# A two-layer decoder trunk on one core: input pieces between weight chunks, the second half of q and k two blocks later, and products in column groups

## The chip, the cores and the metric

The kernel runs on one core of one Trainium2 chip. A core has TensorE (PE, with its weight loads as PEld), VectorE (DVE), ScalarE (ACT), GpSimd (POOL) and SyncE (SP, which here only issues DMAs). The metric is the device time of one execution in microseconds. Before the change the median of 3 runs is 256.97 us (256.9 to 258.04).

## What is computed

Input and output are x of 1 x 256 x 1024 in f32. Two layers are applied one after another; each is one RMS norm, one input projection, two groups of heads side by side, and one output projection onto the residual:

```python
def hybrid_layer(x, norm_g, w_in, conv_w, conv_b, rg_wr, rg_br, rg_wi, rg_bi, rg_lam,
                 q_g, k_g, pe_k, w1_k, w2_k, pe_v, w1_v, w2_v, w_out):
    h = rms_norm(x, norm_g)
    z = h @ w_in
    ...
    y_a = rg_lru(causal_depthwise_conv(rg_x, conv_w, conv_b), rg_wr, rg_br, rg_wi, rg_bi, rg_lam)
    y_a = y_a * jax.nn.silu(rg_gate)
    y_b = nsa(q, k_c, v_c, k_s, v_s, k_w, v_w, br_gate, q_g, k_g,
              pe_k, w1_k, w2_k, pe_v, w1_v, w2_v)
    y_b = y_b * jax.nn.silu(nsa_gate)
    y = jnp.concatenate([y_a, y_b], axis=-1)
    return x + y @ w_out
```

`rg_lru` is a gated linear recurrence over the 256 tokens (512 channels). `nsa` is attention of 8 query heads on 2 key/value heads with three branches: compressed blocks (keys and values through a small MLP), selected blocks and a sliding window, each a masked softmax, mixed by sigmoid gates. q and k are normalised by head and partly rotated.

## The kernel before, in words

Everything is kept with channels on partitions and the 256 tokens in the free dimension, apart from q, k and v, which are made with tokens on partitions (two halves of 128). Each f32 operand of a large product is split into a high part that TensorE takes as fp32r and a low part, the rest; `mm3` (L170 to L173) issues three products for each tile: high by high, and the two mixed ones. The high part of a weight chunk (`wh`) is cast by ACT from the loaded `raw` (L165) or, for chunks with `dma=True`, by a DMA that POOL issues (L156); the low part (`wl`) is a subtraction on DVE (L166).

The weights come in 33 chunks a layer, and the program walks over them as steps: 8 of `tm1` (q, k and the keys, two token halves by 2 x 384 columns, so 12 products of 128 x 384 each), 2 of `cmp_prod`, 3 of `tm2` (values and gates), 12 of `fm` (blocks x0 to x3, n0, n1, g0 to g3, n2, n3, each 24 products of 128 x 256), and 8 of `out_proj`. A step has work placed before it, in its middle and after it. `SL` says ahead of which fm block the attention's parts stand: `qk` for `qk_transpose` of the two token halves, `cmp` for the compressed MLP (`cmp_act`, `cmp_kv`, `cmp_kt`), `att` for the scores and `turn`, `aout` for transposes and outputs, `gates` for the recurrence. `ahead(n)` says how many chunks beyond the next are cast and split early. From that the framework makes one instruction order per engine; PE, DVE, ACT, POOL and SP each run theirs in order and wait for each other by semaphores. PSUM has the pools s (3 banks), fm (2), pp (2) and m (1).

What the change touches:

- The start: `x_load` (L98) issues pieces of x on SP, between `Chunk.load` (L145) of the first chunks; chunk 0 comes in two halves. PE runs eight warm-up products (L113) meanwhile. `first_x(k)` makes piece k of h: the scaled high part on ACT (L213), the low part on DVE (L214), the square for the norm on ACT (L219, L222) and its addition on DVE (L223). `softplus` (L186 to L207) is a chain of small DVE steps. `rms1` needs the sum of all squares (L305), then DVE (L306 to L310) and POOL's power (L177); after it come `norm_sums` and `norm_rope`, which lead to q and k.
- `qk_transpose(t)`: two transposes of k on PE (L366), four copies on ACT (L370, L371) and two subtractions on DVE (L372, `kl`), then four transposes of q (L375), two copies (L379), two subtractions (L380, `qs`) and one copy (L382, `qT`). The scores (L570 to L572) of token half 0 need half 0 alone; those of half 1 need both. `cmp_hid` (L454) and `cmp_act` (L463 to L467: product, tanh `hth` on ACT, `hs` on DVE) lead to `cmp_kv` (L472, L473).
- `att_out(i)`: products with the values of the two branches, in groups of 64 columns (L619, L622), then one 128-wide product with the compressed values (L624), then DVE's product with the gate. It runs four times a layer.

```python
def ahead(n):
    return 0 if n < 4 else 1 if n < 7 else 2 if n % 33 < 14 or n % 33 > 26 else 1
...
    for n in range(RAWB):
        upto("load", n + 1)
        if n < 3:
            x_load(*((1, 3), (3, 5), (5, 8))[n])
```

Of the kernel before, what the change touches and what calls it, by code (L numbers as in the profile page):

```python
# [2 lines left out]

# [1 line left out]

# [5 lines left out]
F32 = mybir.dt.float32  # L11
# [3 lines left out]
AF = mybir.ActivationFunctionType  # L15
ALU = mybir.AluOpType
AX = mybir.AxisListType

P = 128
# [19 lines left out]
for _n, _w in (("g", 8), ("cw", 16), ("cb", 4), ("br", 4), ("bi", 4), ("lam", 4)):  # L39
# [10 lines left out]
PRB = 6  # L50

K = dict(scale="A", ev1="A", hid="A", pct="A")
SL = dict(qk=(0, 0), order=("x0", "x1", "x2", "x3", "n0", "n1", "g0", "g1", "g2", "g3", "n2", "n3"),
          cmp=(2, 3, 4), att=(1, 3, 3, 4, 6, 7, 10, 11), turn=(2, 4, 5, 6, 8, 10,
          12, 13), cs=(5, 5), cpt=6, aout=(6, 7, 12, 15), gates=(2, 3, 4, 5), tab=6, sqrt=5,
          scan=8, rout=(9, 11))
# [1 line left out]


def ahead(n):  # L60
    return 0 if n < 4 else 1 if n < 7 else 2 if n % 33 < 14 or n % 33 > 26 else 1

# [7 lines left out]
def hybrid_trunk_kernel(ctx: ExitStack, tc: tile.TileContext, vx, wc, wt, wv, wf, wo, w1, w2, pe,  # L72
# [56 lines left out]
    mhalf = cp.tile([P, 1], F32, name="mhalf")  # L129
    G.memset(mhalf, -0.5)  # L130
    warm = cp.tile([P, 1], F32, name="warm")
    A.activation(warm, ones, AF.Tanh)
    identb = cp.tile([P, P], BF16, name="identb")
    maskb = cp.tile([P, P], BF16, name="maskb")

# [1 line left out]
    class Chunk:  # L137
        def __init__(self, src, k, n, parts=1, dma=False):
            self.src, self.k, self.n, self.parts, self.dma = src.rearrange("p k n -> p (k n)"), k, n, parts, dma

        def cuts(self):
            w = self.k * self.n // self.parts
            return [slice(q * w, (q + 1) * w) for q in range(self.parts)]

        def load(self):  # L145
            self.raw = wp.tile([P, WCH], F32, name="raw", tag="raw", bufs=RAWB)[:, :self.k * self.n]
            for c in self.cuts():
                nc.sync.dma_start(self.raw[:, c], self.src[:, c])

        def high(self):  # L150
            self.wh = wp.tile([P, WCH], F32R, name="wh", tag="wh", bufs=WHB)[:, :self.k * self.n]
# [6 lines left out]
        def split(self):  # L158
            if not self.dma:
                self.high()  # L160
            hi = self.wh
            lo = wp.tile([P, WCH], F32R, name="wl", tag="wl", bufs=WLB)[:, :self.k * self.n]
            for c in self.cuts():
                if not self.dma:
                    A.copy(hi[:, c], self.raw[:, c])  # L165
                V.tensor_tensor(lo[:, c], self.raw[:, c], hi[:, c].bitcast(F32), op=ALU.subtract)  # L166
            self.hi, self.lo = (z.rearrange("p (k n) -> p k n", k=self.k) for z in (hi, lo))


# [84 lines left out]
    def layer(l, prev):  # L254
# [8 lines left out]
        def begin():  # L263
            if l == 0:
                L.h, L.sq = h_tiles(), act([P, S], "pct")
            else:
                L.h, L.sq = prev.nh, prev.nsq
            L.rc = act([P, 5, 4], "rc")
            L.rb = act([P, 2, S], "rb")
            L.acc1 = [(bank("s", 3), bank("s", 3)), (bank("s", 3), bank("pp", 2))]  # L270
            L.accc = bank("fm", 2)
            L.qT = act([P, 4, S], "qT")
            L.qs = act([P, 8, S], "qs", 1, F32R)
            L.kd = act([P, 2, 2, S], "kd2", 1, F32R)
            L.vv = act([P, NT, 2, P], "vv")
            L.gate = act([P, NT, 4, 2, 3], "gate")

        def first_x(k):
            h_split(0, L.h, k)
            if k == 2:  # L280
                nc.sync.dma_start(cst, consts)
                L.ga = tables(0)
            if k == 4:
                V.tensor_copy(identb, ident)
                V.tensor_copy(maskb, cview("mask"))
                L.tabs = tables2(L.ga)
            if k:
                sq_add(L.sq, k)
            if k == 5:
                L.sp = softplus()  # L290

# [69 lines left out]
        def qk_transpose(t):  # L361
            zn = L.zn[t]
            tok = slice(t * P, (t + 1) * P)
            pk = bank("pp", 2)
            for i in range(2):
                T.transpose(pk[:, i * P:(i + 1) * P],  # L366
                            zn[:, 8 + 2 * i:10 + 2 * i].rearrange("p h d -> p (h d)"), ident)
            for g in range(2):
                src = pk[g * HD:(g + 1) * HD, :2 * P].rearrange("p (b s) -> p b s", s=P)
                A.copy(L.kd[:HD, g, :, tok], src)  # L370
                A.copy(L.kd[HD:, g, :, tok], src)  # L371
                V.tensor_tensor(kl[:HD, g, :, tok], src, L.kd[:HD, g, :, tok].bitcast(F32), op=ALU.subtract)  # L372
            pq = bank("pp", 2)
            for i in range(4):
                T.transpose(pq[:, i * P:(i + 1) * P], zn[:, 2 * i:2 * i + 2].rearrange("p h d -> p (h d)"),  # L375
                            ident)
            for g in range(2):
                src = pq[g * HD:(g + 1) * HD].rearrange("p (i s) -> p i s", s=P)
                A.copy(L.qs[:HD, g::2, tok], src)  # L379
                V.tensor_tensor(L.qs[HD:, g::2, tok], src, L.qs[:HD, g::2, tok].bitcast(F32),  # L380
                                op=ALU.subtract)
            A.copy(L.qT[:, :, tok], pq.rearrange("p (i s) -> p i s", s=P))  # L382


# [229 lines left out]
        def att_out(i):  # L614
            pt = L.pts.pop(i)
            yb = L.yb = bank("m", 1)
            for b in range(2):
                for g in range(2):
                    T.matmul(yb[g * HD:(g + 1) * HD, :S], L.vv[:, 0, b, g * HD:(g + 1) * HD],  # L619
                             pt[:, g, b, 0:2].rearrange("p a s -> p (a s)"), start=(b == 0), stop=False)  # L620
                for g in range(2):
                    T.matmul(yb[g * HD:(g + 1) * HD, P:S], L.vv[:, 1, b, g * HD:(g + 1) * HD],  # L622
                             pt[:, g, b, 2], start=False, stop=False)
            T.matmul(yb[:, :S], L.vcb[:, 2 * i:2 * i + 2].rearrange("p g d -> p (g d)"), L.pct,  # L624
                     start=False, stop=True)
            yt = act([P, S], "tmp", 3)
            V.tensor_tensor(yt, yb[:, :S], L.sgn[:, i], op=ALU.mult)
            y_split(4 + i, yt)
# [157 lines left out]
        for i in range(2):  # L786
            at(SL["rout"][i], rg_out, 2 * i, mid=True)
        for n, (kind, j) in enumerate(order):
            step(Chunk(wf[l, base[kind] + j], KT, P, dma=n >= 4), R(fm, 0 if kind == "x" else j % 2),
                 F(post[kind], j), *plan[n])  # L790
        for half in range(2):
            for n in range(4):
# [7 lines left out]
        prev0 = prev0 or prev  # L800
        steps += st_
    ch = [s_[0] for s_ in steps]
    done = dict(load=0, cast=0, split=0)

    def upto(what, n):
        while done[what] < min(n, len(ch)):
            getattr(ch[done[what]], what)()
            done[what] += 1

    for n in range(RAWB):  # L810
        upto("load", n + 1)
        if n < 3:
            x_load(*((1, 3), (3, 5), (5, 8))[n])
    for n, (c, run, after, before, middle) in enumerate(steps):
        if n == 0:
            before[0]()
            before[2]()
            before = []
            upto("split", 1)
            sq_add(prev0.sq, 0)  # L820
        for f in before:
            f()
        if n < 4:
            upto("split", n + 2)
        upto("load", min(n + LOAD + 1, done["split"] + RAWB))
        upto("cast", n + CAST + 1)
        for f in middle:
            f()
        run(c)
        if after:  # L830
            after()
        upto("split", n + 2 + ahead(n))
# [108 lines left out]
```

## Time and profile before

| | before |
|---|---|
| median of 3 runs | 256.97 us |
| the profiled execution, its own time | 256.85 us |
| span in the profile | 255.1 us |
| PE busy | 245.7 us, 96% |
| PEld busy | 226.4 us, 89% |
| DVE busy | 198.0 us, 78% |
| ACT busy | 164.8 us, 65% |
| POOL busy | 41.3 us, 16% |
| moved by DMA | 57.17 MB, mean 224 GB/s |

The span is the time between the first and the last event of the profiled execution; the execution's own time is 1.75 us more. Busy time of PE counts matmuls whose ends are modelled, and weight loads (PEld) run beside them. The page's share of an engine is an average over stages, so the stages are read from the timeline and from windows.

### The profile page before, as it was taken

The page shows a single profiled execution, that of the slowest core. Times are in us where ns is not written, and L with a number is a line of the kernel's source. Part 1 is how long each engine was busy: PE and PEld are TensorE (multiplying, and loading weights), DVE is VectorE, ACT ScalarE, POOL GpSimd, SP SyncE. Part 2 cuts the span into 40 slices and gives each one's busy share as a digit, 9 for nine tenths or more (in the row PEclk, how much of TensorE's full clock was granted, in tenths as well). Part 3 has the DMA queues.
Part 4 walks back from the last instruction along what each step waited for, and adds up shares of the span by engine and source line. Part 5 has one row for each costly group of instructions (what it writes and reads, how often), then busy time and mean ns, then how long its engine had stood idle before and what let it go on. Part 6 is the DMA issues. An engine that isn't in the chain of part 4 may idle for free.

```text
span 255.1 us, 5220 instructions
## 1 busy us (share of the span) xinstructions
PE 245.7 (96%) x1954; PEld 226.4 (89%) x1954; DVE 198.0 (78%) x398; ACT 164.8 (65%) x419; POOL 41.3 (16%) x65
## 2 busy tenths in 40 slices
PE   8799998999999999999999999899999999999994
PEld 4699998898988998999999999688898979989993
DVE  4897789999978988754995569997986998865422
ACT  5966439889999878622864444679799896951000
POOL 0027461001800011100001053101100001010000
PEclk9999999999999999999999999999999999999999
DMA  6988999865794798662469868784457366842022
GB/s 203 335 272 282 350 416 363 303 177 211 247 328 166 247 279 276 176 197 76 156 220 360 296 218 252 274 297 168 163 169 226 130 220 237 272 154 82 3 82 82
DMA packets 17449, 57.17 MB, mean 224 GB/s; under 512 B 2192, under 2 KB 3088, under 8 KB 16912
## 3 DMA queue, kind: packets, MB, share of 16 engines
q1 hardware_dynamic: 12816, 40.06, 45.4%
q0 software_dynamic: 4608, 16.78, 21.3%
q8 instruction: 15, 0.25, 0.4%
q14 instruction: 10, 0.08, 0.1%
HBM read 55.78 MB, written 1.05 MB: 223 GB/s over the span
## 4 chain that ended last, share of the span: by engine, by line
PE 84%; DVE 8%; DMA 2%; ACT 2%; POOL 2%; issue 1%; SPq 0%; DVEq 0%; POOLq 0%
PE fm L173 14%; PE fm L171 14%; PE fm L172 14%; PE s L172 5%; PE s L171 4%; PE s L173 4%; PE pp L609 4%; PE m L619 3%; DVE wl L166 3%; PE fm L648 3%; PE s L570 2%; PE m L624 2%; DMA head<-in_vx_dram 2%; PE s L571 2%; PE m L622 1%; PE pp L171 1%
## 5 line engine op out<-in xcount | busy, mean ns | idle before, releaser
L166 DVE TENSOR_TENSOR wl<-raw,wh 128x1024 fp32r<-128x1024 f32 (+4 forms) x67 | 74.3, 1115 | 9.8 <-PE fm L173 4.6
L173 PE MATMUL fm<-hh,wl 128*128 128x256 f32 x192 | 55.8, 291 | 0.7 <-DVE wl L166 0.7
L171 PE MATMUL fm<-hh,wh 128*128 128x256 f32 x192 | 56.3, 293 | 0.0
L172 PE MATMUL fm<-hl,wh 128*128 128x256 f32 x192 | 55.3, 288 | 0.0
L165 ACT CAST wh<-raw 128x768 fp32r<-128x768 f32 (+4 forms) x35 | 30.8, 886 | 28.8 <-DMA raw<-in_wc_dram 7.0
L173 PEld LDWEIGHTS fm<-hh,wl 128*128 128x128 f32 x192 | 36.7, 191 | 1.4 <-DVE wl L166 0.9
L171 PEld LDWEIGHTS fm<-hh,wh 128*128 128x128 f32 x192 | 36.8, 192 | 0.3
L172 PEld LDWEIGHTS fm<-hl,wh 128*128 128x128 f32 x192 | 36.7, 191 | 0.1
L171 PE MATMUL fm<-yy,wh 128*128 128x256 f32 x96 | 27.7, 289 | 0.0
L583 ACT ACTIVATE pr<-s,sm 128x128 f32<-128x128 f32 (+1 forms) x64 | 26.2, 421 | 1.6 <-DVE sm L575 0.8
L173 PE MATMUL fm<-yy,wl 128*128 128x256 f32 x96 | 26.8, 279 | 0.0
L172 PE MATMUL fm<-yy,wh 128*128 128x256 f32 x96 | 26.8, 279 | 0.0
L596 ACT ACTIVATE pr<-pr,sm 128x128 f32<-128x128 f32 (+1 forms) x64 | 24.1, 454 | 1.9 <-DVE sm L589 1.9
L156 POOL DMA_DIRECT2D wh<-in_wo_dram x16 | 8.5, 530 | 68.4 <-PE fm L173 40.1
L172 PEld LDWEIGHTS fm<-yy,wh 128*128 128x128 f32 x96 | 18.1, 188 | 0.1
L171 PEld LDWEIGHTS fm<-yy,wh 128*128 128x128 f32 x96 | 18.1, 188 | 0.1
L173 PEld LDWEIGHTS fm<-yy,wl 128*128 128x128 f32 x96 | 18.0, 188 | 0.0
L171 PE MATMUL s<-wh,hh 128*128 128x384 f32 x48 | 16.0, 357 | 1.7 <-ACT wh L165 1.7
L156 POOL DMA_DIRECT2D wh<-in_wf_dram x16 | 9.0, 565 | 50.4 <-PE fm L173 26.9
L714 DVE TENSOR_TENSOR head<-head,fm 128x512 f32<-128x512 f32 x11 | 7.5, 685 | 12.1 <-PE fm L173 12.1
L172 PE MATMUL s<-wl,hh 128*128 128x384 f32 x48 | 16.4, 342 | 0.1
L173 PE MATMUL s<-wh,hl 128*128 128x384 f32 x48 | 16.1, 335 | 0.0
(202 smaller groups left out, 627.1 us busy)
## 6 DMA issues: line engine op xcount, KB each, us to landing
raw<-in_wf_dram SPq DMA_DIRECT2D x24, 512.0 KB, 4.8
wh<-in_wf_dram POOLq DMA_DIRECT2D x16, 512.0 KB, 4.4
raw<-in_wo_dram SPq DMA_DIRECT2D x16, 512.0 KB, 4.6
wh<-in_wo_dram POOLq DMA_DIRECT2D x16, 512.0 KB, 4.3
raw<-in_wt_dram SPq DMA_DIRECT2D x15, 384.0 KB, 3.5
yy<-in_w_dram SPq DMA_DIRECT2D x4, 1024.0 KB, 7.7
raw<-in_wc_dram SPq DMA_DIRECT2D x4, 512.0 KB, 5.1
raw<-in_wv_dram SPq DMA_DIRECT2D x4, 420.0 KB, 4.6
```

Source lines behind the costliest of these rows:

```text
L156: G.dma_start(self.wh, self.src)
L165: A.copy(hi[:, c], self.raw[:, c])
L166: V.tensor_tensor(lo[:, c], self.raw[:, c], hi[:, c].bitcast(F32), op=ALU.subtract)
L171: T.matmul(o, lh, rh, start=start, stop=False)
L172: T.matmul(o, lh, rl, start=False, stop=False)
L173: T.matmul(o, ll, rh, start=False, stop=stop)
L583: A.activation(pr[g][:, b], ov[:, b], AF.Exp, bias=sm[:, 0, 2 * g + b:2 * g + b + 1], accum_out=sm[:, 1, 2 * g + b:2 * g + b + 1])
L596: A.activation(pr[g][:, b], pr[g][:, b], AF.Copy, scale=sc_)
L609: T.transpose(pp[:, (2 * g + b) * P:(2 * g + b + 1) * P], pr[g][:, b, c * P:(c + 1) * P], ident)
L619: T.matmul(yb[g * HD:(g + 1) * HD, :S], L.vv[:, 0, b, g * HD:(g + 1) * HD], pt[:, g, b, 0:2].rearrange("p a s -> p (a s)"), start=(b == 0) ...
L648: T.matmul(pg[:, e * S:(e + 1) * S], L.rws[:, j, e], cx[:, j], start=True, stop=True)
L714: V.tensor_tensor(x_sb[:, m], x_sb[:, m], os_[0].rearrange("p (a s) -> p a s", a=2), op=ALU.add)
```

## The change

1. At the start, the first half of chunk 0 is issued on ACT's queue, ahead of the warm-up tanh. x comes in smaller pieces on SP: (0,1), half chunk, (1,2), chunk 1, (2,3), chunk 2, (3,5), chunk 3, (5,8), chunk 4.
2. The squares for the norm are taken later: pieces 0 to 7 at k = 2, 3, 3, 4, 5, 6, 7, 7 in place of each at its own k.
3. `qk=(0, 2)`: the second token half's `qk_transpose` stands before fm block x2 instead of x0.
4. `ahead` ends its value 2 at chunk 12 of a layer instead of 14, and the low parts of fm blocks 2 and 3 (4 and 5) are ordered on DVE behind the last `qs` of token half 0 (1).
5. The last product of `att_out` is issued as two groups of 64 columns.

```diff
-SL = dict(qk=(0, 0), order=("x0", "x1", "x2", "x3", "n0", "n1", "g0", "g1", "g2", "g3", "n2", "n3"),
+SL = dict(qk=(0, 2), order=("x0", "x1", "x2", "x3", "n0", "n1", "g0", "g1", "g2", "g3", "n2", "n3"),
...
-    return 0 if n < 4 else 1 if n < 7 else 2 if n % 33 < 14 or n % 33 > 26 else 1
+    return 0 if n < 4 else 1 if n < 7 else 2 if n % 33 < 12 or n % 33 > 26 else 1
...
-    A.activation(warm, ones, AF.Tanh)
...
+            self.after = None
...
-        def load(self):
+        def load(self, first=False):
             self.raw = wp.tile([P, WCH], F32, name="raw", tag="raw", bufs=RAWB)[:, :self.k * self.n]
-            for c in self.cuts():
-                nc.sync.dma_start(self.raw[:, c], self.src[:, c])
+            for q, c in enumerate(self.cuts()):
+                (A if first and q == 0 else nc.sync).dma_start(self.raw[:, c], self.src[:, c])
...
-                V.tensor_tensor(lo[:, c], self.raw[:, c], hi[:, c].bitcast(F32), op=ALU.subtract)
+                done = self.after() if self.after else None
+                with tc.issue_after(done.ins) if done else nullcontext():
+                    V.tensor_tensor(lo[:, c], self.raw[:, c], hi[:, c].bitcast(F32), op=ALU.subtract)
...
-            if k:
-                sq_add(L.sq, k)
+            for j in {2: [0], 3: [1, 2], 4: [3], 5: [4], 6: [5], 7: [6, 7]}.get(k, []):
+                sq_add(L.sq, j)
...
-                V.tensor_tensor(L.qs[HD:, g::2, tok], src, L.qs[:HD, g::2, tok].bitcast(F32),
-                                op=ALU.subtract)
+                L.qk_done[t] = V.tensor_tensor(L.qs[HD:, g::2, tok], src, L.qs[:HD, g::2, tok].bitcast(F32),
+                                               op=ALU.subtract)
...
-            T.matmul(yb[:, :S], L.vcb[:, 2 * i:2 * i + 2].rearrange("p g d -> p (g d)"), L.pct,
-                     start=False, stop=True)
+            for g in range(2):
+                T.matmul(yb[g * HD:(g + 1) * HD, :S], L.vcb[:, 2 * i + g], L.pct, start=False, stop=True)
...
-            step(Chunk(wf[l, base[kind] + j], KT, P, dma=n >= 4), R(fm, 0 if kind == "x" else j % 2),
+            c = Chunk(wf[l, base[kind] + j], KT, P, dma=n >= 4)
+
+            if n in (2, 3, 4, 5):
+                c.after = (lambda t: lambda: L.qk_done[t])(0 if n < 4 else 1)
+            step(c, R(fm, 0 if kind == "x" else j % 2),
...
-    done = dict(load=0, cast=0, split=0)
+    ch[0].load(True)
+    A.activation(warm, ones, AF.Tanh)
+    done = dict(load=1, cast=0, split=0)
...
-    for n in range(RAWB):
+    for n in range(1, RAWB):
+        x_load(*((1, 2), (2, 3), (3, 5))[n - 1])
         upto("load", n + 1)
-        if n < 3:
-            x_load(*((1, 3), (3, 5), (5, 8))[n])
+    x_load(5, 8)
...
-            sq_add(prev0.sq, 0)
```

How the instructions move. First SP's queue at the start of the program, before (head is the tile that holds the vectors and x; 256 columns are one piece of x):

```order
L100 DMA head<-in_vx_dram 128x336
L148 DMA raw<-in_wt_dram 128x384 x2
L100 DMA head<-in_vx_dram 128x512
L148 DMA raw<-in_wt_dram 128x768
L100 DMA head<-in_vx_dram 128x512
L148 DMA raw<-in_wt_dram 128x768
L100 DMA head<-in_vx_dram 128x768
L148 DMA raw<-in_wt_dram 128x768 x4
```

and now:

```order
L100 DMA head<-in_vx_dram 128x336
L148 DMA raw<-in_wt_dram 128x384
L100 DMA head<-in_vx_dram 128x256
L148 DMA raw<-in_wt_dram 128x768
L100 DMA head<-in_vx_dram 128x256
L148 DMA raw<-in_wt_dram 128x768
L100 DMA head<-in_vx_dram 128x512
L148 DMA raw<-in_wt_dram 128x768
L100 DMA head<-in_vx_dram 128x768
L148 DMA raw<-in_wt_dram 128x768 x3
```

One half of chunk 0 is gone from SP (it is on ACT's queue), and chunk 1 (the first 128 x 768) stands behind one further piece of x instead of two.

Second, DVE in layer 1 around the q,k stage, before:

```order
L166 TENSOR_TENSOR wl<-raw,wh 128x1024 x2
L400 TENSOR_SCALAR gate<-gate 128x24
L166 TENSOR_TENSOR wl<-raw,wh 128x1024
L400 TENSOR_SCALAR gate<-gate 128x24
L372 TENSOR_TENSOR kl<-pp,kd_1771 64x2x128
L380 TENSOR_TENSOR qs<-pp,qs 64x4x128
L372 TENSOR_TENSOR kl<-pp,kd_1771 64x2x128
L637 TENSOR_TENSOR xpad_71<-fm,rb 128x256
L380 TENSOR_TENSOR qs<-pp,qs 64x4x128
L166 TENSOR_TENSOR wl<-raw,wh 128x1024
```

and now (line numbers are by 2 to 4 higher: kl L375, qs L383, wl L168, xpad L640):

```order
L403 TENSOR_SCALAR gate<-gate 128x24 x2
L375 TENSOR_TENSOR kl<-pp,kd_1776 64x2x128
L383 TENSOR_TENSOR qs<-pp,qs 64x4x128
L375 TENSOR_TENSOR kl<-pp,kd_1776 64x2x128
L640 TENSOR_TENSOR xpad_71<-fm,rb 128x256
L383 TENSOR_TENSOR qs<-pp,qs 64x4x128
L168 TENSOR_TENSOR wl<-raw,wh 128x1024
L643 SCALAR_TENSOR_TENSOR cx<-xpad_71,head,cx 128x256
L168 TENSOR_TENSOR wl<-raw,wh 128x1024
```

The three low parts that stood ahead of the first kl are those of blocks x2, x3 and n0; x2's and x3's now stand behind the first token half's four steps, and n0's behind the second half's.

Third, ACT in the same stage, before (kd and qs are copies of k and q, hid and hth belong to the compressed MLP, L583 are exponentials of scores, L638 is the convolution's first step):

```order
L379 CAST qs<-pp 64x4x128
L370 CAST kd_1771<-pp 64x2x128
L371 CAST kd_1771<-pp 64x2x128
L83 COPY hid<-m 128x128
L379 CAST qs<-pp 64x4x128
L382 COPY qT<-pp 128x4x128
L583 ACTIVATE pr,sm<-s,sm 128x128 x4
L638 ACTIVATE cx<-xpad_72,head 128x256
L465 ACTIVATE hth<-m 128x160
L651 ACTIVATE rr<-fm,hb 128x256
L596 ACTIVATE pr<-pr,sm 128x128 x4
```

and now (L586 exponentials, L599 their scaling, L468 hth):

```order
L641 ACTIVATE cx<-xpad_71,head 128x256
L385 COPY qT<-pp 128x4x128
L83 COPY hid<-m 128x128
L586 ACTIVATE pr,sm<-s,sm 128x128 x4
L373 CAST kd_1776<-pp 64x2x128
L641 ACTIVATE cx<-xpad_72,head 128x256
L599 ACTIVATE pr<-pr,sm 128x128 x4
L374 CAST kd_1776<-pp 64x2x128
L382 CAST qs<-pp 64x4x128
L468 ACTIVATE hth<-m 128x160
L373 CAST kd_1776<-pp 64x2x128
```

The second half's copies stand behind the first tile's exponentials, and hth behind the scaling and three of these copies.

## Rows read from the trace of the kernel before

**Rows 1.** The page, parts 1 and 4: busy time by engine; the chain by engine.

```profile
PE 245.7 (96%) x1954; PEld 226.4 (89%) x1954; DVE 198.0 (78%) x398; ACT 164.8 (65%) x419; POOL 41.3 (16%) x65
...
PE 84%; DVE 8%; DMA 2%; ACT 2%; POOL 2%; issue 1%; SPq 0%; DVEq 0%; POOLq 0%
```

**Rows 2.** Waits of PE, first and last of six: us in total, times, longest.

```profile
PE s L171 <- ACT wh L165: 1.7, 1, 1.7
...
PE m L527 <- DVE sc L521: 0.3, 1, 0.3
```

**Rows 3.** The page's GB/s by slice, DMA issues to 24 us, timeline at the start.

```profile
GB/s 203 335 272 282 350 416 363 303 177 211 247 328 166 247 279 276 176 197 76 156 220 360 296 218 252 274 297 168 163 169 226 130 220 237 272 154 82 3 82 82
...
raw<-in_wt_dram SPq DMA_DIRECT2D x7, 384.0 KB, 5.3
...
6.99 0.51 ACT L213 ACTIVATE hh<-head 128x256 fp32r<-128x256 f32 x1 [1.85 <-DMA head<-in_vx_dram]
...
7.26 0.34 PE L173 MATMUL pp<-wh,hl 128*128 128x384 f32 x1
...
9.28 0.79 PE L171 MATMUL s<-wh,hh 128*128 128x384 f32 x3 [1.68 <-ACT wh L165]
```

**Rows 4.** Timeline of DVE from 7 us, and PE before the first fm block.

```profile
7.53 0.48 DVE L214 SCALAR_TENSOR_TENSOR hl<-head,hh 128x256 fp32r<-128x256 f32 x1 [1.59 <-ACT hh L213]
...
20.89 2.10 DVE L166 TENSOR_TENSOR wl<-raw,wh 128x768 fp32r<-128x768 f32 x2
23.52 0.16 DVE L306 TENSOR_SCALAR rc<-m 128x4 f32<-128x4 f32 x1 [0.53 <-PE m L305]
...
40.53 0.39 PE L173 MATMUL fm<-hh,wl 128*128 128x256 f32 x1 [0.67 <-DVE wl L166]
```

**Rows 5.** Timeline of layer 1's q,k stage, by engine; ACT at 180 us.

```profile
159.82 2.34 DVE L166 TENSOR_TENSOR wl<-raw,wh 128x1024 fp32r<-128x1024 f32 x2
...
163.38 0.41 DVE L372 TENSOR_TENSOR kl<-pp,kd 64x256 fp32r<-64x256 f32 x1
...
163.56 0.41 PE L454 MATMUL m<-yy,zz 128*32 128x128 f32 x2
165.18 0.41 PE L366 MATMUL pp<-cst,pt 128*128 128x128 f32 x2 [1.22 <-DVE kl L372]
165.52 1.52 PE L454 MATMUL m<-yy,zz 128*32 128x128 f32 x48
167.52 0.66 PE L375 MATMUL pp<-cst,pt 128*128 128x128 f32 x4 [0.48 <-ACT qT L382]
...
168.68 0.38 PE L570 MATMUL s<-kd,qs 128*128 128x256 f32 x1
...
180.48 0.47 ACT L651 ACTIVATE rr<-fm,hb 128x256 f32<-128x256 f32 x1 [1.55 <-PE fm L648]
```

**Rows 6.** Windows: us, PE, PEld, DVE, ACT, POOL busy, PE clock, DMA share, GB/s.

```profile
58.00:78.00 20.00, 19.85 (x153) 17.97 (x151) 18.40 (x50) 19.38 (x62) 7.14 (x12) 1.00 0.79 266
180.00:200.00 20.00, 19.75 (x151) 17.95 (x150) 16.54 (x47) 19.49 (x64) 1.63 (x3) 1.00 0.60 189
```

**Rows 7.** Timeline of ACT in layer 0: copies of the second token half.

```profile
48.18 0.37 ACT L370 CAST kd<-pp 64x256 fp32r<-64x256 f32 x1
...
48.96 0.58 ACT L379 CAST qs<-pp 64x512 fp32r<-64x512 f32 x1
```

**Rows 8.** Timeline of PE: the last products of att_out, at two places.

```profile
78.69 0.60 PE L619 MATMUL m<-pt,vv 128*64 128x256 f32 x4
79.12 0.39 PE L622 MATMUL m<-pt,vv 128*64 128x128 f32 x4
...
80.10 0.28 PE L173 MATMUL fm<-hh,wl 128*128 128x256 f32 x1
...
81.62 0.65 PE L619 MATMUL m<-pt,vv 128*64 128x256 f32 x4
...
82.42 0.28 PE L171 MATMUL fm<-hh,wh 128*128 128x256 f32 x1
```

More of the change, by code (lines that the diff above doesn't have):

```diff
@@ L1 @@
 import math
-from contextlib import ExitStack
+from contextlib import ExitStack, nullcontext
 import numpy as np
@@ L276, in begin @@
             L.gate = act([P, NT, 4, 2, 3], "gate")
+            L.qk_done = {}
         def first_x(k):
```

## Prediction

> **What bounds the kernel now.** I read the page first: PE is busy 96% of the span and carries 84% of the chain that ended last [rows 1]. So a part of the change is worth what it takes off PE's work or off PE's waits. The waits view lists only six waits of PE, from 1.7 us down to 0.3 [rows 2]; with the idle time that the timeline shows between small matmuls, a few us in 255 are all that waiting can give back. Then I looked at three stretches, one for each place that the change touches.
>
> In the **start**, chunk 0's last product issues at 7.26 and the next product of PE at 9.28, 1.68 us after PE ran dry [rows 3]. It waits for the cast of chunk 1. ACT itself waited 1.85 us for x until 6.99, and the weight transfers of this stage take a median of 5.3 us from issue to landing [rows 3]. But look at DVE: from 7.53, where its wait of 1.59 us ends, it works nearly without a gap until the two low parts from 20.89 are done at 22.99, and its next instruction, the norm's first step, runs at 23.52 [rows 4]. From there a chain of small steps of DVE and POOL ends in PE's wait of 0.67 us before 40.53, where the first fm block lacks a low part [rows 4]. So PE has slack before 40.5, and DVE sets when layer 0 really gets going.
>
> In **layer 1's q,k stage** the rows are plain [rows 5]. DVE runs three low parts from 159.82 before it comes to the first kl at 163.38. PE starts the compressed-MLP products (L454, 64 passes) at 163.56, stops for 1.22 us before the second half's transposes at 165.18, for 0.48 before those at 167.52, and comes to the first scores at 168.68. Those 5.12 us hold 64 passes at 1.52/48 = 0.032, so 2.03, and transposes of 0.41 + 0.66 = 1.07; the other 2.0 us are waiting.
>
> In the **attention stages** ACT is the second limit: 19.38 of 20 us busy from 58 to 78, 19.49 of 20 from 180 to 200 [rows 6]. Just before the second stretch it sat idle for 1.55 us until PE delivered at 180.48 [rows 5]. A gain made earlier in layer 1 can be kept up to about that idle time plus the 0.51 left in the stretch, 2.1 us in all; beyond it ACT takes it back.
>
> **The change, part by part.**
>
> *Start (x in pieces, first half on ACT's queue, squares behind).* Bytes are the same; what moves is order. Before, two x pieces in one request lay ahead of chunk 1's weights, which were requested fourth and by the median of 5.3 us landed near 8; now one piece of 128 KB goes behind them. At the 203 GB/s that the first slice of the span moved [rows 3], 128 KB are 0.63 us, so chunk 1 lands near 7.3. A square and a second pair of x steps on ACT no longer stand ahead of its cast either. If the gate of everything were PE, 1.68 us would go. But the gate is DVE, whose block of 15.5 us from 7.53 to 22.99 keeps its instructions: the squares' additions are only moved. Chunk 1's low part and the second hl now come in another order, and the block begins when x(1,2) is there. Two causes pull back: the small softplus steps, spread out before, now stand in a row at the end, just ahead of the norm, and cost more than their own length when each waits for the last; and the requests for the chunks behind it are cut into more pieces on SP. I take 0.4 us off the time, nearest to what the DVE rows allow; the ends are 1.2 (the whole 1.59 us gap but for the reordering) and −0.3 (transfers come in as before, and the softplus tail is longer). What PE gains beyond that, it spends waiting at 40.53. The half chunk on ACT's queue adds one issue to ACT and takes one from SP; I cost it at nothing, because ACT's first work waits for x anyway; without that cover it would be one issue late, inside the 0.3 of the upper end.
>
> *Second half of q,k two blocks on; low parts behind q,k; ahead 12.* In layer 1 DVE's 3.56 us of low parts (159.82 to 163.38) no longer stand before kl. The first half's four steps then run as soon as ACT has cast, before 165. PE does its 64 passes without a stop, 163.56 + 2.03 = 165.6, and scores can start there instead of at 168.68. Of these 3.1 us, 1.07 is only moved, and 2.0 is waiting that goes. What is late next: on ACT the tanh of the compressed MLP now stands behind three copies of the second half (0.37, 0.37, 0.58: 1.3 us [rows 7]) and the four scalings of the first tile, and DVE's hs behind two of its steps; PE's L472 products and the larger scores wait for them. ACT had idle time there [rows 5], so I charge half of the 1.3: 0.7. Net 1.3 us gained, ends 0 (all of it comes back with the scalings) and 2.0. The low parts of blocks x2 and x3 then follow the first half's steps, 1.2 us each (half of the 2.34 at 159.82); PE wants them only after the scores and the whole x1 block, so x1 is their cover. If that were gone, a wait of up to 1.2 before x2 would take the place of the one removed. The smaller ahead moves a load and a cast of the last projection chunks one step later; the low part that was early is not wanted sooner, so nothing.
>
> In layer 0 the same move has little to remove: the waits view shows no wait of PE in its q,k stage. But the second half's seven copies, four of 0.37 and three of 0.58, so 3.2 us, go from about 50 us into the stretch where ACT is 19.38 of 20 busy [rows 6, 7]. The half that stays also gets DVE earlier. I take 0, with ends −0.5 (gain) and +2.6 (3.2 less the 0.62 free).
>
> *The last product of att_out as two column groups.* In the trace the groups before it keep PE's pace: four full passes take 79.12 − 78.69 = 0.43, and 0.21 for the four half-length ones [rows 8]. Today's wide product starts after that, and the next fm product but one stands at 80.10, 0.98 after 79.12. In the other place the row of four groups is left directly for fm: from 81.62 to the second fm product at 82.42 are 0.80 [rows 8]. With the new form the same sequence is 0.21 + 0.80 = 1.01. So one change of form goes, two more passes come, and nothing is left: 0, with an end of +0.3 (eight times 0.03).
>
> The Trainium skill, page "TensorEngine Tiling (Array Packing)", section "Tiling Modes", says that changing the tiling mode drains TensorE; the long steps before 80.10 and 82.42 agree with it. The same page's section "Overview" allows up to twice the speed where one dimension is at most 64; the L619 rows do not show it, and it is rival (b) below.
>
> **Sum**, against the profiled execution (256.85, close to the median of 256.97): 256.85 − 0.4 − 0 − 1.3 − 0 = 255.15, so 255.1. About 0.5%, or 1.3 us, is what a measurement of this kernel can tell from no change.
>
> **The rivals.**
>
> (a) *The waits go whole.* Start −1.2, layer 0 −0.5, layer 1 −2.1 as far as ACT's idle time lets it: 253.1. For it: DVE's gap of 1.59 and PE's idle time are real. Against it: it needs ACT to take the late copies everywhere without delay. Chance 0.20.
>
> (b) *The two column groups run side by side.* Then two of the four passes of 0.107 vanish at eight places: 8 × 0.21 = 1.7 more, 253.4. Against it: four passes of L619, which are such pairs already, took 0.43, one pass after another. Chance 0.05. It is the rule in section "Overview" of the Trainium skill's page "TensorEngine Tiling (Array Packing)".
>
> (c) *Nothing is gained.* The start ends in the same DVE chain and the same low part at 40.5; what layer 1 gains, ACT takes back because the tanh and the later copies are late. Then only half of the start's 0.4 is left: 256.6. For it: ACT is full in both attention stages, and the 0.67 us wait shows that PE's early start buys nothing there. Chance 0.22.
>
> (d) *Slower, by layer 0's late copies.* If the second half's copies, in the stretch where ACT is full, hold up the scores of the second tile, up to 2.6 us come on top; with 0.4 and 0.9 gained elsewhere, 256.85 + 2.6 − 1.3 = 258.2. It decides if ACT has not finished the last qT of layer 0 by about 58. Against it: the copies come before the full stretch's first scalings if PE reaches x2 in time. Chance 0.08.
>
> The forecast keeps 0.45. **How the numbers follow.** The forecast's own range is 254.2 to 256.4 from its terms. (a) and (b) stretch the low end to 252.9, (c) the high end to 257.2; (d) and the tails are left out. Faster by over 1.3 us: three quarters of the forecast (0.34) and all of (a) and (b): 0.59, so 0.6. Same: the rest of the forecast and (c): 0.33, so 0.32. Slower: 0.08.
>
> **What would show it.** In the changed profile: PE's idle time before its first product of chunk 1 under 1 us, and the norm's first step at 23.1 instead of 23.52; the wait before the first fm block still there, and longer. In layer 1, L454's successor in one piece without idle time inside, scores at about 165.6 after the shift, and a new idle time of PE before L472's successor under 1.2 us. ACT still full from 180 to 200. att_out's eight places as long as now. Wrong would be: a norm step later than 23.5, an idle time of PE over 1.5 us in layer 0's second q,k half or before its larger scores, or PE's busy time falling by over 1 us, which would speak for column groups side by side.

## The result and the profile after

| | before | changed | ratio, 95% interval |
|---|---|---|---|
| first comparison | 256.99 us (4 runs) | 254.15 us (4 runs, 253.69 to 254.65) | 0.9881 [0.9846, 0.9915] |
| once more, on another occasion | 256.64 us (9 runs) | 254.55 us (5 runs, 253.86 to 254.91) | 0.991 [0.9894, 0.9926] |
| span of the profiled execution | 255.1 us | 252.7 us | |
| PE busy | 245.7 us | 244.9 us | |
| ACT busy | 164.8 us | 164.6 us | |
| POOL busy | 41.3 us | 38.3 us | |

The kernel became faster by 2.1 to 2.8 us, about 1%. The prediction was 255.1, within 252.9 to 257.2. No engine has less to do: the counts of instructions are those of before, with 16 products more on PE. POOL's 38.3 us are the same 65 instructions, some of them shorter in this execution, and PE's busy time, whose ends are modelled, is 0.8 us lower. PE's idle time fell from 9.4 to 7.8 us, 1.6 of the 2.4 us by which the span fell, so the gain lies for the greater part in waits. The page of the changed kernel, parts 1 and 4 (the chain now runs for 13% over DVE and 10% over ACT, against [rows 1]):

```profile
PE 244.9 (97%) x1970; PEld 224.2 (89%) x1970; DVE 196.6 (78%) x398; ACT 164.6 (65%) x419; POOL 38.3 (15%) x65
...
PE 69%; DVE 13%; ACT 10%; DMA 2%; issue 2%; POOL 1%; SPq 1%; DVEq 0%; ACTq 0%; POOLq 0%
```

The waits view of PE (us in total, times, longest; before, [rows 2]). Line numbers here are 2 to 4 higher than before. The waits for the cast of chunk 1 (1.7), for kl in the transposes (1.2) and for qT (0.5) are gone; new are those of the probabilities' transposes L612, which need a PSUM bank that the late kl still reads, and of L475, which needs hs:

```profile
PE pp L612 <- DVE kl L375: 1.1, 2, 0.9
PE m L113 <- DVE wz L110: 1.1, 1, 1.1
PE m L475 <- DVE hs L470: 0.8, 1, 0.8
PE s L174 <- DVE wl L168: 0.5, 2, 0.3
PE s L573 <- ACT pr L586: 0.3, 1, 0.3
```

Timeline of the start (to be laid beside [rows 3]): chunk 1's weights end ACT's wait at 6.55, and PE goes from chunk 0's last product at 7.14 to chunk 1's first at 7.44 without a pause, where it had stood still for 1.68 us.

```profile
6.55 0.83 ACT L165 CAST wh<-raw 128x768 fp32r<-128x768 f32 x1 [0.31 <-DMA raw<-in_wt_dram]
...
7.14 0.34 PE L175 MATMUL pp<-wh,hl 128*128 128x384 f32 x1
...
7.44 0.79 PE L173 MATMUL s<-wh,hh 128*128 128x384 f32 x3
```

The norm (beside [rows 4]): the products for it on PE, DVE's first step, POOL's two powers, and the low part of block x0 on DVE. The norm's products had begun at 22.51 before, so PE is 0.93 earlier here; DVE's step is 0.48 earlier, and x0's low part is there before PE asks for it, so that PE's wait of 0.67 us before the first fm block [rows 4] is gone in this execution.

```profile
21.58 0.97 PE L308 MATMUL m<-ones,pct 128*128 128x1 f32 x8
...
23.04 0.15 DVE L309 TENSOR_SCALAR rc<-m 128x4 f32<-128x4 f32 x1
...
28.72 4.50 POOL L179 TENSOR_TENSOR st<-st,mhalf 128x12 f32<-128x12 f32 x2 [4.35 <-DVE st L336]
...
37.67 1.23 DVE L168 TENSOR_TENSOR wl<-raw,wh 128x1024 fp32r<-128x1024 f32 x1
```

Layer 1's q,k stage (beside [rows 5]), DVE, PE, ACT, DVE, PE. kl runs at 160.16 and the low parts of x2 and x3 from 164.13, behind it; PE does the 64 passes in one piece and comes to the scores at 164.25. The tanh hth stands behind the scaling L599 and the late copies until 172.37, hs until 173.22, and PE waits 0.81 for it.

```profile
160.16 0.42 DVE L375 TENSOR_TENSOR kl<-pp,kd 64x256 fp32r<-64x256 f32 x1 [0.43 <-ACT kd L374]
...
164.13 1.23 DVE L168 TENSOR_TENSOR wl<-raw,wh 128x1024 fp32r<-128x1024 f32 x1
...
162.37 1.96 PE L457 MATMUL m<-yy,zz 128*32 128x128 f32 x64
164.25 0.39 PE L573 MATMUL s<-kd,qs 128*128 128x256 f32 x1
...
170.19 1.28 ACT L599 ACTIVATE pr<-pr,sm 128x128 f32<-128x128 f32 x4
172.37 0.29 ACT L468 ACTIVATE hth<-m 128x160 f32<-128x160 f32 x1
...
173.22 0.32 DVE L470 SCALAR_TENSOR_TENSOR hs<-hth,m 128x160 f32<-128x160 f32 x1
...
173.59 0.30 PE L475 MATMUL m<-w2s,hs 128*32 128x64 f32 x2 [0.81 <-DVE hs L470]
```

Layer 0, where the second half's kl is late by 0.88 us for L612, and the two windows of [rows 6]:

```profile
52.35 0.63 PE L612 MATMUL pp<-cst,pr 128*128 128x128 f32 x4 [0.88 <-DVE kl L375]
...
58.00:78.00 20.00, 19.70 (x158) 17.62 (x157) 19.65 (x51) 19.05 (x62) 6.34 (x11) 1.00 0.70 240
180.00:200.00 20.00, 19.92 (x156) 17.13 (x155) 18.79 (x48) 18.71 (x55) 1.63 (x3) 1.00 0.65 210
```

From 180 to 200 ACT is no longer full (18.71 against 19.49).

The column groups at the place of [rows 8], first row: from the last narrow groups' start at 77.77 to the second fm product at 78.75 are 0.98 us, as the 0.98 before.

```profile
77.34 0.60 PE L622 MATMUL m<-pt,vv 128*64 128x256 f32 x4
77.77 0.39 PE L625 MATMUL m<-pt,vv 128*64 128x128 f32 x4
77.99 0.60 PE L628 MATMUL m<-pct,vcb 128*64 128x256 f32 x4
...
78.75 0.28 PE L174 MATMUL fm<-hl,wh 128*128 128x256 f32 x1
```

Followed along the program, PE stands earlier than before by 0.93 at the norm (21.58 against 22.51), 1.21 at the first transposes of layer 1 (158.52 against 159.73), and 2.30 at the last att_out (233.43 against 235.73). So in these two executions 1.2 us come from the start with layer 0, and 1.1 from layer 1.

### The profile page after: what moved, and what is told of

It is laid out like the page before. It is cut to its first block, busy times and chain, and to the rows that moved or that the text cites. A ratio compares the mean times of both kernels' runs of the same rounds, so it can differ in the third digit from the quotient of the medians.

```text
span 252.7 us, 5257 instructions
## 1 busy us (share of the span) xinstructions
PE 244.9 (97%) x1970; PEld 224.2 (89%) x1970; DVE 196.6 (78%) x398; ACT 164.6 (65%) x419; POOL 38.3 (15%) x65
## 4 chain that ended last, share of the span: by engine, by line
PE 69%; DVE 13%; ACT 10%; DMA 2%; issue 2%; POOL 1%; SPq 1%; DVEq 0%; ACTq 0%; POOLq 0%
PE fm L173 13%; PE fm L175 13%; PE fm L174 12%; DVE wl L168 5%; PE pp L612 4%; PE m L622 3%; PE s L173 3%; PE s L174 3%; PE s L175 3%; DMA raw<-in_wt_dram 2%; ACT pr L586 2%; PE m L625 1%; PE s L573 1%; PE m L628 1%; PE m L510 1%
## 5 line engine op out<-in xcount | busy, mean ns | idle before, releaser
L168 DVE TENSOR_TENSOR wl<-raw,wh 128x1024 fp32r<-128x1024 f32 (+4 forms) x67 | 74.5, 1117 | 9.0 <-PE pp L174 3.1
L173 PE MATMUL fm<-hh,wh 128*128 128x256 f32 x192 | 57.1, 297 | 0.1
L175 PE MATMUL fm<-hh,wl 128*128 128x256 f32 x192 | 54.9, 286 | 0.1
L586 ACT ACTIVATE pr<-s,sm 128x128 f32<-128x128 f32 (+1 forms) x64 | 26.0, 417 | 8.2 <-DVE sm L580 5.9
L599 ACT ACTIVATE pr<-pr,sm 128x128 f32<-128x128 f32 (+1 forms) x64 | 24.0, 455 | 4.2 <-DVE sm L592 4.1
L612 PE MATMUL pp<-cst,pr 128*128 128x128 f32 x96 | 15.2, 275 | 1.1 <-DVE kl L375 1.1
```

Source lines behind the costliest of these rows:

```text
L173: T.matmul(o, lh, rh, start=start, stop=False)
L175: T.matmul(o, ll, rh, start=False, stop=stop)
L586: A.activation(pr[g][:, b], ov[:, b], AF.Exp, bias=sm[:, 0, 2 * g + b:2 * g + b + 1], accum_out=sm[:, 1, 2 * g + b:2 * g + b + 1])
L599: A.activation(pr[g][:, b], pr[g][:, b], AF.Copy, scale=sc_)
L612: T.transpose(pp[:, (2 * g + b) * P:(2 * g + b + 1) * P], pr[g][:, b, c * P:(c + 1) * P], ident)
```

## The experiments

The parts, each alone on the kernel before or taken out of the changed kernel. The first four ran together, with the kernel before at 256.63 us (29 runs), the next four with 256.78 (11 runs), the last four with 256.64 (9 runs).

**e3_groups: column groups alone.**

```diff
-            T.matmul(yb[:, :S], L.vcb[:, 2 * i:2 * i + 2].rearrange("p g d -> p (g d)"), L.pct,
-                     start=False, stop=True)
+            for g in range(2):
+                T.matmul(yb[g * HD:(g + 1) * HD, :S], L.vcb[:, 2 * i + g], L.pct, start=False, stop=True)
```

> The kernel before with the column groups alone. Theory A: no change, 257.0 within 0.3, the stretch from the last narrow group to the second fm product as long as before. Theory C (groups side by side): 255.3.

256.86 us, ratio 1.001 [0.999, 1.0029]. Theory C is out: no gain and no loss can be told.

**e1_start: the start alone** (edits 1 and 2).

> The kernel before with the start of the change alone (x in pieces, half chunk on ACT's queue, squares behind). Theory A (each part pays by itself, and the start is the largest single term): the products for the norm on PE come at about 21.6 instead of 22.5, and of these 0.9 us between 0.9 and 1.5 are left at the end: 255.4 to 256.1. Theory B (the norm's chain on DVE and POOL takes it back, as the prediction had it; the changed kernel keeps it only because the q,k part also frees DVE): 0.4 gained, 256.6.

256.21 us, ratio 0.998 [0.995, 1.0011]. The 12 runs fall into two parts: six lie between 255.44 and 255.90 us, in theory A's range, and six between 256.53 and 260.42. The one that was profiled took 258.67 us (span 256.9, against 255.1 before), so it shows how the gain can be lost, not the usual course; no profile of a run of the first part was taken. PE was 1.6 us ahead at the norm (20.89) and at the first transposes (37.08). It lost all of that and more in layer 0's q,k stage. ACT and DVE there:

```profile
43.91 1.04 ACT L165 CAST wh<-raw 128x1024 fp32r<-128x1024 f32 x1 [1.75 <-DMA raw<-in_wf_dram]
...
45.76 0.43 DVE L375 TENSOR_TENSOR kl<-pp,kd 64x256 fp32r<-64x256 f32 x1 [1.83 <-ACT kd L374]
```

ACT waits 1.75 us for the weights of block x3, and its cast stands ahead of the second copy pair of k, so kl comes at 45.76. The waits view gives PE's side:

```profile
PE pp L369 <- DVE kl L375: 3.5, 2, 2.3
```

Then something more: the windows of the same stretch (PE, PEld, DVE, ACT, POOL busy, then the granted clock, DMA share and GB/s).

```profile
44.00:46.00 2.00, 0.03 (x1) 0.00 (x0) 0.24 (x1) 1.94 (x4) 0.00 (x0) 1.00 1.09 416
46.00:48.00 2.00, 1.64 (x9) 1.36 (x10) 1.79 (x4) 1.95 (x6) 0.00 (x0) 0.74 0.79 294
48.00:50.00 2.00, 2.00 (x11) 2.00 (x11) 1.13 (x2) 0.79 (x2) 0.00 (x0) 0.50 0.30 56
50.00:52.00 2.00, 2.00 (x17) 2.00 (x16) 1.82 (x4) 1.37 (x4) 0.00 (x0) 0.91 0.66 250
```

PE is idle from 44 to 46 (0.03 busy), and the granted clock is 0.74 of full in the next window, 0.50 in the one after that, and 0.91 in the last: at 0.50 TensorE runs at its lower level of 1.2 GHz. In the kernel before, whose longest waits of PE were 1.68 and 1.22 us, all windows from 42 to 52 stand at 1.00. The wait of 2.3 us so cost more than 2.3: PE came to layer 0's first scores 1.69 us ahead of the kernel before (43.53 against 45.22) and to layer 1's first transposes 1.96 us behind it (161.69 against 159.73). The DMA share is 1.09 in the window where PE stands: the DMA engines are full, and x3's weights are what is late.

**e2_qk: the q,k part alone** (edits 3 and 4).

> The kernel before with the q,k part alone (second half two blocks on, low parts behind q,k, ahead 12). Theory A: layer 1 gains 1.1 us, layer 0 between -0.3 and +0.5: 255.5 to 256.2. Theory B (it also unloads DVE ahead of the first fm block): the wait of 0.67 us before the first fm block goes as well, and 1.8 are gained: 255.2.

254.97 us, ratio 0.9928 [0.9904, 0.9952]: 1.7 us. In its profile PE is 0.83 ahead at layer 1's first transposes, which it already was at the norm (0.80, the start's transfers having come in earlier in this execution), and 1.98 at the last att_out. So in this execution layer 0 gives nothing and layer 1 gives 1.15, theory A's path, although the time lies below theory A's range and beside theory B's 255.2. Theory B's own sign did not come: the wait before the first fm block is still there (0.7).

**e4_qk_nogate and w1_qk_ahead12: which piece of edit 4.** Both have `qk=(0, 2)` on the kernel before, without the queueing of low parts; they differ in one number:

```diff
-    return 0 if n < 4 else 1 if n < 7 else 2 if n % 33 < 14 or n % 33 > 26 else 1
+    return 0 if n < 4 else 1 if n < 7 else 2 if n % 33 < 12 or n % 33 > 26 else 1
```

> The kernel before with the second half of q,k two blocks on, but with the low parts' old order and ahead 14. If the place of the transposes is what counts, as e2: 255.5 to 256.2. If DVE's low parts ahead of the first kl are what held the scores in layer 1, the scores there still wait for kl until about 164 to 166 and no more than 0.5 us is gained: 256.5 to 257.

> The kernel before with the second half of q,k two blocks on and ahead 12, no queueing, old start, no column groups. It differs from e4_qk_nogate (no gain) in the number 12 alone. If ahead carries the q,k part, 1.5 to 2.2 us faster than before. If the queueing is needed with the old start, under 0.6 us faster.

e4_qk_nogate: 257.05 us, 1.0016 [0.9996, 1.0037]. w1_qk_ahead12: 254.94 us, 0.9934 [0.9921, 0.9946]. With the second half moved, the number 12 decides between no gain and 1.7 us, and the queueing adds nothing that can be told (e2_qk had 0.9928). DVE and PE in layer 1 of e4_qk_nogate:

```profile
159.81 2.34 DVE L169 TENSOR_TENSOR wl<-raw,wh 128x1024 fp32r<-128x1024 f32 x2
...
162.15 1.22 DVE L169 TENSOR_TENSOR wl<-raw,wh 128x1024 fp32r<-128x1024 f32 x1
...
163.36 0.41 DVE L376 TENSOR_TENSOR kl<-pp,kd 64x256 fp32r<-64x256 f32 x1
...
165.37 0.39 PE L574 MATMUL s<-kd,qs 128*128 128x256 f32 x1
...
176.07 0.63 PE L613 MATMUL pp<-cst,pr 128*128 128x128 f32 x4 [1.75 <-DVE kl L376]
```

and of w1_qk_ahead12:

```profile
159.63 1.21 DVE L169 TENSOR_TENSOR wl<-raw,wh 128x1024 fp32r<-128x1024 f32 x1
...
161.24 0.42 DVE L376 TENSOR_TENSOR kl<-pp,kd 64x256 fp32r<-64x256 f32 x1 [0.24 <-ACT kd L375]
...
165.32 0.39 PE L574 MATMUL s<-kd,qs 128*128 128x256 f32 x1
...
173.68 0.63 PE L613 MATMUL pp<-cst,pr 128*128 128x128 f32 x4 [0.56 <-DVE kl L376]
```

With 14, three low parts (159.81 to 163.36) stand ahead of the first kl as in [rows 5]; with 12 one does, and kl comes at 161.24 instead of 163.36. But this first kl is not what PE waits for: PE comes to the first scores at 165.37 and at 165.32, in both kernels 3.3 us earlier than before (168.68; 1.07 of it are the transposes that now stand behind). The low parts are felt further on. With 14, DVE's reduction of these scores (L581) starts at 168.39 instead of 167.10, ACT's exponentials at 169.12 instead of 167.81, the second half's copies of k behind them at 172.81 instead of 169.44, and the last kl at 175.50 instead of 173.11; for that kl the probabilities' transposes L613 wait, 1.75 us instead of 0.56. So moving the transposes alone brings the scores forward and loses it again at L613: from layer 1's first transposes to the last att_out e4_qk_nogate gains nothing on the kernel before (0.08 us ahead, then 0.06 behind), w1_qk_ahead12 gains 1.7 (0.13 to 1.83). The number 12 with both halves left ahead of x0 and without the queueing was not run.

**u4_nogate and w2_nogate: the changed kernel without the queueing** (the same kernel, on two occasions; `if n in ():` in place of `if n in (2, 3, 4, 5):`), beside **w0_after**, the changed kernel again.

> The changed kernel without the queueing of low parts behind q,k (ahead 12 stays). If the queueing carries the gain, one low part stands ahead of the second kl on DVE again and 0.5 to 1.2 us are lost: 254.7 to 255.4. If the smaller ahead carries it, within 0.3 of the changed kernel: 254.0 to 254.5.

> The changed kernel without the queueing of low parts once more, on the same chip as w0_after. If the queueing does nothing, the two agree within 0.4 us. If it costs (it holds t1's copies and hs back, 0.8 us of PE's wait in layer 1), this one is 0.5 to 1.2 us faster than w0_after.

> The changed kernel once more, beside the two next to it on one chip. Its gain over the kernel before stays at 2.6 to 3.2 us, a ratio of 0.988 to 0.990.

u4_nogate 253.42 us, 0.9877 [0.986, 0.9894]; w2_nogate 253.9, 0.9879 [0.9857, 0.9901]; w0_after 254.55, 0.991 [0.9894, 0.9926]. w0_after's gain of 2.1 us is below the 2.6 that was expected, and u4_nogate lies below both of its ranges. The queueing brings nothing; without it the kernel is 0.65 us faster in the median of the same occasion, though the intervals still touch. The profiles say where: from layer 1's first transposes to the last att_out, PE gains 1.1 us on the kernel before with the queueing (0.97 to 2.13 in w0_after) and 1.7 without (2.37 to 4.08 in w2_nogate). The waits view of w2_nogate has no wait for hs:

```profile
PE m L113 <- DVE wz L110: 1.1, 1, 1.1
PE pp L612 <- DVE kl L375: 0.7, 2, 0.6
PE s L173 <- ACT wh L165: 0.4, 1, 0.4
PE s L573 <- DVE qs L383: 0.3, 1, 0.3
PE s L174 <- DVE wl L168: 0.3, 1, 0.3
```

On the same occasion w1_qk_ahead12 took 254.94 us. It differs from w2_nogate in the start and in the column groups, and the groups are worth nothing (e3_groups): so on top of the q,k part the start is worth 1.0 us (0.9934 against 0.9879, the intervals apart).

**u6_qk00: the changed kernel with both halves ahead of x0 again.**

> The changed kernel with both token halves of q,k ahead of x0 again; the low parts stay queued behind q,k. If moving the second half is what pays, PE's waits for kl and qT in layer 1 (1.22 and 0.48 us before) come back and about 1.1 us of the gain goes: 255.3 to 255.8. If it is the order of the low parts on DVE, the time stays within 0.4 of the changed kernel: 253.8 to 254.6, with PE's wait for hs in layer 1 (0.8 us in the changed kernel) gone.

255.1 us, 0.994 [0.9928, 0.9952], between the two ranges. Moving the second half is worth about 1 us of the whole, once the low parts are out of the way (0.8 to 1.5 by the two ratios of the changed kernel). The wait for qT is back, that for hs is gone, and that for kl in the transposes came back as 0.3 us, not 1.22:

```profile
PE fm L175 <- DVE wl L168: 0.9, 1, 0.9
PE pp L378 <- ACT qT L385: 0.5, 1, 0.5
```

**u3_start_cast4: the start alone, POOL's cast DMAs one chunk later** (`LOAD, CAST = 6, 4`).

> As e1_start (the start alone), with POOL's cast DMAs asked for one chunk later. Theory D: the start's gain is lost in layer 0 because POOL, done earlier with the norm's powers, sends its cast DMAs earlier; they share the full DMA engines with block x3's weights, whose cast on ACT stands ahead of the second half of kd. Then x3's weights land before 42.5 instead of 43.84, PE's wait for kl there falls from 2.3 us to under 1, and the start keeps about 1 us: 255.4 to 255.8 in the median. Rival: the DMA engines are full anyway, whatever the order, and ACT still waits over 1.5 us for x3: 256.2 as e1_start.

259.53 us, 1.011 [1.0092, 1.0128], a miss in time. The first line below is ACT's cast of x3 in layer 0: it starts at 42.54 after 0.50, so the weights did land before 42.5, and PE's wait for kl in that place fell to 0.2. But the number moved the order of layer 1 as well, where PE now stands 3.94 us for kl (second line):

```profile
42.54 1.06 ACT L165 CAST wh<-raw 128x1024 fp32r<-128x1024 f32 x1 [0.50 <-DMA raw<-in_wf_dram]
...
166.75 0.66 PE L369 MATMUL pp<-cst,pt 128*128 128x128 f32 x2 [3.94 <-DVE kl L375]
```

The clock fell there as well, to a mean of 0.72 from 164 to 170. Theory D fits the place it spoke of, in one profiled execution, but is not shown by it: POOL's first DMA went out 1.0 us later than in e1_start (33.84 against 32.84) because its powers took 5.48 us instead of 4.50 this time, so the number is not the only difference. As a cure it is worthless, and how much of e1_start's median it explains stays open. The Trainium skill, page "DMA: Bandwidth & Descriptors", section "Queues, rings and completion order", says that each DMA engine takes packets from its queue rows in turn. That fits e1_start, where x3's weights, requested on SP at 32.39, took 11.4 us to land, and the first of POOL's two DMAs, from 32.84, took 7.6; no run here shows the turns themselves.

**u1_oldsq: the changed kernel with each square at its own k.**

> The changed kernel with each square at its own k again. If the pieces of x alone carry the start, within 0.3 of the changed kernel: 254.0 to 254.5. If the squares ahead of the casts count, the products for the norm come 0.4 to 0.9 us later than the changed kernel's 21.58 and 254.6 to 255.1 results.

253.88 us, 0.9885 [0.987, 0.99]. In its profile the norm's products begin at 21.89, 0.31 later than in the changed kernel's, and later than in all eight profiles with the squares behind (20.58 to 21.58). But the time is not longer: no gain of the squares' place can be told, and the start's gain goes with the pieces of x.

**x1_turn3: the first transposes of probabilities one block later, without the queueing** (`turn=(3, 4, 5, ...`).

> The changed kernel without the queueing, with the first transposes of probabilities (turn) one block later. They wait for the PSUM bank that the late kl frees, 0.7 us in all in u4_nogate. If that wait goes and nothing takes its place, 0.3 to 0.7 us faster than w2_nogate. If ACT, full from 58 on, takes it back, the same or up to 0.5 us slower.

253.7 us, 0.9882 [0.9867, 0.9897]: as w2_nogate. The waits of L612 fell from 0.7 to 0.2 us and those of the scores for qs rose from 0.3 to 0.8: a wait that was exchanged.

## Why the prediction was right, and where its steps were not

**The bound** was read rightly: PE's work stayed, and the gain lies for the greater part in its waits. **The forecast's time** was 1.0 us too high in the first comparison, 0.6 in the second. The first, 254.15, lies at the fast edge of the forecast's own range, 254.2 to 256.4, and within the stated range by what rival (a) adds to it. How that own range follows from the ends of the terms, which add up to 253.15 on the fast side, the prediction does not say. Of its signs, the norm's step (23.04) and hs's wait came; the wait before the first fm block came in one of the two profiles of the changed kernel; ACT from 180 to 200, forecast full, was not (18.71). By its terms:

*Start, 0.4 forecast.* Mis-sized: 0.4 in the median alone (e1_start), 1.0 on top of the q,k part (w2_nogate against w1_qk_ahead12). DVE's norm step came at 23.04, for which 23.1 was forecast, and PE went without its pause. The sentence that failed is "What PE gains beyond that, it spends waiting at 40.53": PE kept 1.56 us up to the scores of layer 0 (43.66 against 45.22), because x0's low part was ready at 38.9. A part of that is luck and no merit of the change: POOL's two powers in the chain between took 4.50 us, where before they took

```profile
29.21 5.48 POOL L177 TENSOR_TENSOR st<-st,mhalf 128x12 f32<-128x12 f32 x2 [4.36 <-DVE st L333]
```

In w0_after, the same kernel, they took 5.48 again, and the predicted wait of PE before the first fm block was there:

```profile
28.41 5.48 POOL L179 TENSOR_TENSOR st<-st,mhalf 128x12 f32<-128x12 f32 x2 [4.36 <-DVE st L336]
...
39.59 0.39 PE L175 MATMUL fm<-hh,wl 128*128 128x256 f32 x1 [0.78 <-DVE wl L168]
```

So the prediction's path is real, and which one is taken changes from execution to execution: the wait stands (0.66 to 0.87 us) in all five profiles whose powers took 5.48, old start or new, and is at most 0.16 in the nine with 4.50. Between profiles with equal powers the start's lead at layer 0's first scores differs too: 0.46 us for the changed kernel against e3_groups (43.66, 44.12), 0.92 for w0_after against the kernel before (44.30, 45.22), 1.55 for w2_nogate against w1_qk_ahead12 (42.69, 44.24). The start alone is worth 0.4 us in the median (e1_start, an interval that reaches no change). In the one execution of it that was profiled, a long one, the gain is lost neither at 40.53 nor in DVE's chain, as the prediction had it, but in ACT's order behind late transfers, which the prediction did not look at. In the changed kernel the cast of x3 stands further back, behind the first half of q,k; that this is why the start's gain is kept there was argued from the order and not tested by itself.

*Layer 1, 1.3 forecast.* 1.1 measured. The pieces came in time: 64 passes without a stop, scores at 164.25 (165.6 forecast, less the 1.21 by which all was earlier), hs late with 0.81 us of waiting (0.7 charged), ACT's four scalings and three late copies ahead of hth. The reason given for them did not hold. The prediction let the scores come early because the low parts no longer stand before kl; in e4_qk_nogate all three still stand there, and the scores come at 165.37 all the same, 3.3 us earlier than before. Moving the transposes does that alone; what the low parts hold up is the second half's kl, and with it L613. That path the prediction did not look at, and that the number came out is in part luck.

*The smaller ahead, "so nothing".* Wrong, and it is the term that mattered most: 2.1 us between the medians of e4_qk_nogate and w1_qk_ahead12, 1.9 at the last att_out of their profiles. What it moves are low parts of the fm blocks (x3 and n0 go behind the first kl), not of the last projection chunks. They were not wanted sooner, true; but they stood on DVE ahead of what was wanted. The prediction ascribed that clearing to the queueing, which on top of the number 12 brings nothing and makes hs late. In the changed kernel the two belong together, since the queueing refers to instructions that must have been issued before the low parts are; with ahead at 14 they are not.

*Layer 0's late half, 0 forecast, up to 2.6 as rival (d).* About +0.35 in the first profile: 1.56 ahead at the first scores, 1.21 at layer 1's first transposes; 0.88 of waiting for kl is the largest piece. ACT from 58 to 78 did not fill up (19.05), so (d) did not come.

*Column groups, 0.* Confirmed by e3_groups and by the rows. Rival (b), which is the rule in section "Overview" of the Trainium skill's page "TensorEngine Tiling (Array Packing)", is out here: four passes in groups of 64 columns keep the pace of 0.11 us each.

*Rivals (a) and (c).* (a), the waits gone whole, with 253.1, is what the kernel without the queueing comes near (253.4 and 253.9), which is not the kernel that was forecast. (c) did not come; e4_qk_nogate shows something like it: the transposes moved, the scores earlier, and the gain taken back by the second half's late copies.

## What to carry to other kernels

Before queueing work behind other work, look how early the unwanted work is issued at all: with the transposes moved, one number that issues two low parts later decided between no gain and 1.7 us, and the explicit order on top cost some. A delay on an engine that is not the bottleneck need not show at the next thing that reads its result: follow it to the place where PE stands. And when two single profiles are compared, see first whether an unchanged instruction, here POOL's powers, took another time in them. When a stage is made to start earlier, follow the in-order queue of every engine behind it to its next DMA wait; in the profiled run of the start alone the gain was lost where a cast that waits for weights stood ahead of copies that PE waits for. The version to keep is the changed kernel without the queueing: 253.4 to 253.9 us.

## What the runs showed of the hardware that was not expected

- After a wait of 2.31 us on PE (e1_start) the windows of 2 us that follow stand at a granted clock of 0.74, 0.50 and 0.91; after one of 3.94 us (u3_start_cast4) the mean from 164 to 170 is 0.72; around a wait of 1.75 us (e4_qk_nogate, 174 to 180) it stands at 1.00.
- POOL's two powers on 128 x 12 in layer 0 took 4.50 us in nine of the fourteen profiled executions and 5.48 in five, with the same code at the same place; in layer 1 each takes 2.26 to 2.30. What decides is not known; the chain before the first fm block is longer by that 1 us.
- With the new order of transfers and squares PE came to the norm's products between 20.58 us (w2_nogate) and 21.58 (the changed kernel's first profile), with the old order between 21.71 (e2_qk) and 22.51 (before): single profiles of one order differ there by 0.8 to 1.0 us, about as much as the term that was to be judged.
